# A two-layer attention encoder on one core: layer A's queries and group 0's keys transposed by VectorE in 32x32 blocks through DRAM, products with v moved between the projections

## The chip, the cores and the metric

The kernel runs on one core of a Trainium2 chip. The metric is the device time of one execution in microseconds (us), as a median of several runs. All matrix work is on TensorE (PE). VectorE (DVE), ScalarE (ACT) and GpSimd (POOL) work beside it, and SyncE (SP) issues almost all DMA transfers.

## The reference, cut to what matters

The input x has 512 tokens of 1024 features, float32. Two layers follow each other, A and then B. Each one normalises x, projects it, applies attention with 16 heads of 64, multiplies by silu of a gate, projects back and adds to x. Layer A, which the change is about, has three dilation groups with queries, keys and values of their own:

```python
proj = hn @ w_in                                     # 1024 -> 3 groups * (q, k, v) * 1024, and a gate of 1024
for g, (window, dilation) in enumerate(((128, 1), (512, 4), (2048, 16))):
    q = rms_norm(qkv[:, :, g, 0], q_gain[g])         # per head, over its 64 elements
    k = rms_norm(qkv[:, :, g, 1], k_gain[g])
    o, lse = dilated_group_attention(q, k, v, bias, dilation, reach)   # q.k/8 + bias, exp, times v
alpha = jax.nn.softmax(jnp.stack(lses), axis=0)      # groups are merged by their denominators
y = jnp.sum(alpha[..., None] * jnp.stack(outs), axis=0) * jax.nn.silu(gate)
x = x + y @ w_out
```

Layer B has one set of queries, keys and values and a two-dimensional neighbourhood; the change leaves it as it is.

## The kernel before, in words

**Numbers.** Every large product is done three times, with operands split in a high and a low part of type float32r (`mm3`, L212). Weights are streamed from DRAM in loads of up to 1024 columns (`raws`, L166, three buffers) and split on the chip: ScalarE casts the high part, VectorE or GpSimd subtracts the low part (`split`, L124, four buffers of each). One such split feeds 12 matmuls of 512 columns.

**Layer A** runs over 8 head pairs (`hc`, L1033). For each pair `main_a` (L474) gives PE, in this order: a projection "rawk" of 512 columns (keys of groups 1 and 2, values of groups 1 and 2), a projection "rawq" of 512 columns (queries of groups 0, 1, 2 and keys of group 0), then v of group 0 and the gate, 128 columns each, which come out transposed already (`project_t`). The first two projections are 96 matmuls each, the last two 24 each. The last pair has rawq ahead of rawk, and the gate of pair 6 is done in pair 7.

In "rawq" and "rawk" tokens lie on partitions: 4 blocks `i` of 128 tokens, and in each the columns. ScalarE evacuates each block with the row's scale (L428), GpSimd squares it (L268), VectorE sums (L269), and the reciprocal root is found by Newton steps, on VectorE for rawq and on GpSimd for rawk. VectorE scales each block in place (`scale`, L281); for rawq of pairs 0 to 5 that is held back in `later` until the gate has been evacuated (L459).

Scores need queries and keys with the head's elements on partitions. `transpose4` (L295) has PE transpose four 128x128 blocks into a PSUM bank. `k_a` (L486) does it twice a pair for the keys of groups 1 and 2. `q_a` (L497) does it four times, for q0, k0, q1 and q2: q0 and k0 are copied and split in high and low parts by ScalarE and VectorE, q1 and q2 are copied by VectorE (L514).

`attn_a` (L656) then forms the scores of a pair in two halves (`scores(u)`), with softmax on VectorE and ScalarE. For all pairs but the last, the softmax weights are transposed off PE already: VectorE transposes them in blocks of 32x32 into the buffer `tr` (L636), four DMAs write that to DRAM and four read it back in another order into `pt` (`turner`, L625). The products with v of a pair (`weigh`, L736) are held in `pending` and done during the next pair, after its first half of scores.

**The order of the work.** PE's order is the program's own. `main` gives the projections, and after each few matmuls `run` (L798) lets `side` emit a piece of attention when it is due: a `yield "wait", key, n` makes the next piece due n ns after the time stamped for that key, counted on a clock of PE's work (`clock`, L198). `later_on` (L226) emits DMAs after a delay on the same clock. A scheduler orders the other engines' instructions, save those that are pinned to the program's order (`keep_in_program_order`). SP's DMAs, weight loads among them, go out one after the other, and one that waits holds up those behind it.

Of the kernel before, what the change touches and what calls it, by code (L numbers as in the profile page):

```python
# [13 lines left out]
F32 = mybir.dt.float32  # L14
F32R = mybir.dt.float32r
I32 = mybir.dt.int32
AF = mybir.ActivationFunctionType
# [25 lines left out]
def tile_hybrid_encoder(  # L43
# [231 lines left out]
    def head_norm(raw, ss, ns, held):  # L275


        rs = wk.tile([P, 32], F32, tag="rs", name="rs")
        rsqrt(nc.vector if ns == 8 else nc.gpsimd, rs[:, : 4 * ns], ss[:, : 4 * ns], 4 * ns, 1.0 / DH)

        def scale():  # L281
            for i in range(4):
                v = raw[:, i, : ns * 64].rearrange("p (a b) -> p a b", b=64)
                m = nc.vector.tensor_mul(
                    v, v, rs[:, i * ns : (i + 1) * ns].unsqueeze(2).to_broadcast([P, ns, 64])
                )
# [16 lines left out]
    def to_tjr(t):  # L303
        return t.rearrange("p (j t r) -> p t j r", t=4, j=4)
# [103 lines left out]
    pq = wk.tile([P, 4096], F32, tag="pt", name="pt", bufs=1)  # L408
    rk = wk.tile([P, 4608], F32, tag="rawk", name="rawk", bufs=1)

    def project_qk(n, ns, key, hc, guard, first=False, **kw):

        box = []

        def evac(i, acc):
            if not box:
                q = key == "rawq"
                if q:
                    box.append(wk.tile([P, 4, n], F32, tag="rawq", name=key, bufs=1))
                else:  # L420
                    o = 4 * n * (hc % (2 if n == 512 else 3))
# [3 lines left out]
            if first:  # L425
                nc.scalar.copy(raw[:, i, :], acc[:, :n])
                return
            nc.scalar.activation(raw[:, i, :], acc[:, :n], AF.Copy, scale=rs_n[:, i : i + 1])  # L428
            squares(raw, ss, i, ns)

        tile_of = lambda hn: lambda k, i: hn[:, k, P * i : P * (i + 1)]
        yield from project(tile_of(hn_h), tile_of(hn_l), n, evac, guard, **kw)
        raw, ss = box
        if first:
            st["first"] = raw, ss
            return
        normed(raw, ss, ns, key, hc)

    def normed(raw, ss, ns, key, hc):
        head_norm(raw, ss, ns, key == "raw" or (key == "rawq" and hc < NHC - 2))  # L440
        st[key, hc] = raw
        stamp[key, hc] = clock[0]

    def first_out():

        raw, ss = st.pop("first")
        for i in range(4):
            nc.scalar.activation(raw[:, i, :], raw[:, i, :], AF.Copy, scale=rs_n[:, i : i + 1])
            squares(raw, ss, i, 4)
        normed(raw, ss, 4, "rawk", 0)  # L450

    def gate_a(hc):
        acc = []
        yield from project_t(acc)
        yield "ya", hc - 2, "y"
        gt = wk.tile([P, S], F32, tag="gt", name="gt", bufs=3)
        eg = wk.tile([P, S], F32, tag="eg", name="eg")
        tc.keep_in_program_order(nc.vector.tensor_mul(tjr(gt), to_tjr(acc[0]), tjr(rs_half)))
        while later:  # L459
            later.pop()()  # L460
        nc.scalar.activation(eg, gt, AF.Tanh)
        gated(hc, gt, eg)

# [20 lines left out]
            yield from gate_a(hc)  # L484

    def k_a(hc):  # L486
        yield "wait", ("rawk", hc), 12500 if hc == 0 else 16000 if hc < NHC - 1 else 10000
        k12 = wk.tile([P, 2, 512], F32, tag="k12", name="k12", bufs=1)
        raw = st.pop(("rawk", hc))
        for g in range(2):  # L490
            tp = transpose4(raw, g * P)
            nc.vector.tensor_scalar(k12[:, g, :], tp, gk[:, g + 1 : g + 2], None, op0=ALU.mult)
            yield
        st["k12", hc] = k12, raw
        stamp["k12", hc] = 0

    def q_a(hc):  # L497
        yield "wait", ("rawq", hc), 15000 if hc < NHC - 2 else 13000
        raw = st.pop(("rawq", hc))
        q0h = wk.tile([P, 512], F32R, tag="q0h", name="q0h", bufs=1)  # L500
        q0l = wk.tile([P, 512], F32R, tag="q0l", name="q0l", bufs=1)
        q12 = wk.tile([P, 2, 512], F32, tag="q12", name="q12", bufs=1)
        k0h = wk.tile([P, EXT], F32R, tag="k0h", name="k0h", bufs=1)
        k0l = wk.tile([P, EXT], F32R, tag="k0l", name="k0l", bufs=1)
        tp = transpose4(raw, 0)
        nc.scalar.copy(tjr(q0h), to_tjr(tp))
        nc.vector.tensor_sub(tjr(q0l), to_tjr(tp), tjr(q0h.bitcast(F32)))
        yield
        tp = transpose4(raw, 3 * P)
        put_k([(trj(k0h[:, 64:EXT]), trj(k0l[:, 64:EXT]), to_trj(tp))], 0)  # L510
        yield
        for g in range(2):
            tp = transpose4(raw, (g + 1) * P)
            nc.vector.tensor_copy(tjr(q12[:, g, :]), to_tjr(tp))  # L514
            yield
        st["q", hc] = q0h, q0l, q12, k0h, k0l
        stamp["q", hc] = 0

    def v_a(hc):

# [135 lines left out]
    def attn_a(hc):  # L656
# [72 lines left out]
        def turn_p(hd, t, pr):  # L729
# [3 lines left out]
            dst = sb(pts[0], at(t, 0, hd, 0), [[32, 4], [512, 4], [1, 32]])  # L733
            nc.vector.tensor_copy(dst, tp.rearrange("p (i a r) -> p i a r", i=4, a=4))

        def weigh():  # L736
            assert not any(t.left for t in turners)
            o = bank("o")
            mms = []
            for g in range(2):  # L740
                for j in range(4):
                    c = 256 + P * g
# [302 lines left out]
    def side():  # L1045
# [20 lines left out]
        for hc in range(NHC):  # L1066
            if hc < NHC - 1:
                yield from k_a(hc)
                yield from chain(q_a(hc), v_a(hc))
                yield from attn_a(hc)  # L1070
                if hc == 2:
                    bias_rows()
            else:
                gap[0] = cycle((500, 500, 700))
                yield from chain(q_a(hc), k_a(hc), attn_a(hc))
        yield from residual(xg)
        stamp["ya", KT - 1, "y"] = 0
        yield "wait", ("x", KT - 1), 800
# [105 lines left out]
```

## Time and profile before

| what | value |
|---|---|
| median of 3 runs | 861.84 us (861.52 to 864.07) |
| the profiled execution | 863.44 us, span 861.7 us |
| mean granted TensorE clock | 0.999 |
| instructions | 15492, on PE 5643 matmuls |
| layer A's share, about 0 to 530 us | one pair takes 66.0 us (200 to 266, 266 to 332) |

The profile's times are in us from the start of the span. In a group's row stand the line, engine, operation, what is written and read, shape and count, then busy time, the mean ns of one and the idle time before it. In a row of the timeline stand the start, the length, the instruction and, in brackets, how long the engine was idle before it and what ended that. In a row of the waits stand who waited for whom, the total, the number of times and the longest.

### The profile page before, as it was taken

To read this page: it belongs to the slowest core of one execution; us is meant where nothing else is said; L and a number is where in the kernel's file an instruction comes from. 1 tells how busy PE (TensorE), PEld (TensorE's weight loads), DVE (VectorE), ACT (ScalarE), POOL (GpSimd) and SP (SyncE) were. 2 spreads that over 40 slices of the span, in tenths; PEclk is the share of its full clock that TensorE was granted. 3 is DMA by queue.
4 is the path that set the end of the run, shared out by engine and by line. 5 is a ranking of instruction groups with operands and counts; after the bars stand their busy time and mean duration, and the time that the engine had idled before them with its cause. 6 is when DMAs were issued, how large, how long until landed. Compare 5 with 4: busy or idle time off the path is not lost.

```text
span 861.7 us, 15492 instructions
## 1 busy us (share of the span) xinstructions
PE 854.2 (99%) x5643; PEld 712.2 (83%) x5643; DVE 513.3 (60%) x1323; ACT 423.1 (49%) x880; POOL 296.2 (34%) x493
## 2 busy tenths in 40 slices
PE   8999999999999999999999999999999999999998
PEld 6788888788788788788788788789988899889786
DVE  6445666566476566566466775538466656766642
ACT  7432653553553553553552564435466645665541
POOL 2351441441541432442342432112444335542411
PEclk9999999999999999999999999999999999999999
DMA  7343565564465464465465274265235664656223
GB/s 247 110 131 108 150 170 157 159 178 137 138 202 156 125 200 130 133 192 148 129 171 175 84 229 105 65 197 179 95 113 149 180 168 145 167 160 174 99 96 124
DMA packets 59707, 128.64 MB, mean 149 GB/s; under 512 B 6384, under 2 KB 23728, under 8 KB 59632
## 3 DMA queue, kind: packets, MB, share of 16 engines
q1 hardware_dynamic: 59344, 127.66, 49.3%
q8 instruction: 44, 0.72, 0.4%
q14 instruction: 31, 0.25, 0.1%
q10 hardware_dynamic: 288, 0.01, 0.0%
HBM read 102.82 MB, written 24.83 MB: 148 GB/s over the span
## 4 chain that ended last, share of the span: by engine, by line
PE 97%; ACT 1%; DVE 1%; DMA 1%; issue 0%; ACTq 0%; DVEq 0%
PE acc L206 82%; PE log L206 5%; PE o L206 5%; PE tp L210 4%; DMA hg<-in_head_gain 1%; ACT p L976 1%; DVE hn_l L368 0%; ACT p L564 0%; ACT rawk L428 0%; ACT wh L127 0%; PE pa L206 0%; PE pl L206 0%; PE pk L206 0%; DVE wl L131 0%; DVE pt L889 0%
## 5 line engine op out<-in xcount | busy, mean ns | idle before, releaser
L127 ACT CAST wh<-wraw 128x512 fp32r<-128x512 f32 (+1 forms) x276 | 161.6, 587 | 298.1 <-PE acc L206 247.4
L206 PE MATMUL acc<-wh,hn_h 128*128 128x512 f32 (+1 forms) x768 | 296.5, 386 | 0.8 <-ACT wh L127 0.7
L206 PE MATMUL acc<-wh,hn_l 128*128 128x512 f32 (+1 forms) x768 | 286.6, 373 | 0.0
L206 PE MATMUL acc<-wl,hn_h 128*128 128x512 f32 (+1 forms) x768 | 286.1, 373 | 0.4 <-DVE wl L131 0.4
L131 POOL TENSOR_TENSOR wl<-wraw,wh 128x512 fp32r<-128x512 f32 (+1 forms) x110 | 137.7, 1252 | 392.9 <-ACT wh L127 342.2
L131 DVE TENSOR_TENSOR wl<-wraw,wh 128x512 fp32r<-128x512 f32 (+1 forms) x166 | 113.2, 682 | 141.5 <-ACT wh L127 137.0
L206 PEld LDWEIGHTS acc<-wh,hn_h 128*128 128x128 f32 x768 | 144.6, 188 | 27.4 <-issue 5.5
L206 PEld LDWEIGHTS acc<-wh,hn_l 128*128 128x128 f32 x768 | 144.6, 188 | 21.1
L206 PEld LDWEIGHTS acc<-wl,hn_h 128*128 128x128 f32 x768 | 144.9, 189 | 19.0 <-DVE wl L131 0.9
L206 PE MATMUL acc<-hn_h,wh 128*128 128x512 f32 x192 | 76.9, 400 | 0.2
L206 PE MATMUL acc<-hn_h,wl 128*128 128x512 f32 x192 | 74.9, 390 | 0.0
L206 PE MATMUL acc<-hn_l,wh 128*128 128x512 f32 x192 | 74.8, 390 | 0.0
L725 ACT ACTIVATE p<-p,mn 128x512 f32<-128x512 f32 (+1 forms) x64 | 44.8, 700 | 53.9 <-DVE mn L714 53.9
L564 ACT ACTIVATE p<-p,mn 128x512 f32<-128x512 f32 (+3 forms) x128 | 69.1, 586 | 0.0
L269 DVE TENSOR_REDUCE ss<-sq 128x4 f32<-128x256 f32 (+1 forms) x96 | 48.4, 504 | 27.3 <-POOL sq L268 26.8
L636 DVE STREAM_TRANSPOSE tr<-p 128x512 f32<-128x512 f32 (+1 forms) x80 | 54.1, 688 | 12.1 <-ACT p L564 10.0
L268 POOL TENSOR_TENSOR sq<-rawk 128x256 f32<-128x256 f32 x64 | 40.5, 640 | 40.5 <-ACT rawk L428 33.5
L206 PE MATMUL acc<-y_h,wh 128*128 128x512 f32 x128 | 52.2, 408 | 0.0
L206 PE MATMUL acc<-y_h,wl 128*128 128x512 f32 x128 | 50.0, 390 | 0.0
L206 PE MATMUL acc<-y_l,wh 128*128 128x512 f32 x128 | 50.0, 390 | 0.0
L206 PEld LDWEIGHTS acc<-hn_h,wh 128*128 128x128 f32 x192 | 36.1, 188 | 9.8 <-ACT rawk L428 2.1
L206 PEld LDWEIGHTS acc<-hn_h,wl 128*128 128x128 f32 x192 | 36.0, 188 | 7.7
(131 smaller groups left out, 1077.8 us busy)
## 6 DMA issues: line engine op xcount, KB each, us to landing
wraw<-in_w SPq DMA_DIRECT2D x95, 512.0 KB
wraw<-in_w SPq DMA_DIRECT2D x38, 384.0 KB
td<-tr SPq DMA_DIRECT2D x56, 256.0 KB
pt<-td SPq DMA_DIRECT2D x56, 256.0 KB
td<-tr SPq DMA_DIRECT2D x24, 224.0 KB
pt<-td SPq DMA_DIRECT2D x24, 224.0 KB
e<-l_d SPq DMA_DIRECT2D x32, 112.0 KB
e<-l_d SPq DMA_DIRECT2D x16, 128.0 KB
```

What stands on the lines that cost most here:

```text
L127: nc.scalar.copy(h, raw)
L131: eng.tensor_sub(l, raw, h.bitcast(F32))
L206: nc.tensor.matmul(o, l, r, **kw)
L210: nc.tensor.transpose(o, i, ident)
L268: nc.gpsimd.tensor_mul(sq, raw[:, i, : ns * 64], raw[:, i, : ns * 64])
L269: nc.vector.tensor_reduce(ss[:, i * ns : (i + 1) * ns], sq.rearrange("p (a b) -> p a b", b=64), axis=AX.X, op=ALU.add)
L564: nc.scalar.activation(pr, pr, AF.Copy, scale=mn[:, 3:4])
L636: nc.vector.transpose(dst, src[:, :n].rearrange("p (i b k) -> p i b k", b=4, k=32))
L725: nc.scalar.activation(row, row, AF.Exp, bias=mn[:, 1:2], scale=-1.0, accum_out=mn[:, 2:3])
L976: nc.scalar.activation(pr[:, o : o + n], pr[:, o : o + n], AF.Exp, bias=mn[:, 0:1], scale=-1.0, accum_out=mn[:, 2:3])
```

## The change

Layer A's rawq is no longer transposed by PE. It is evacuated into a tile of another layout (16 blocks of 32 columns, then 4 blocks of tokens, then 32), scaled at once, and VectorE transposes its 32x32 blocks in place, one instruction for each block of tokens. Four DMAs write the tile to DRAM in pieces of 512 bytes, one for each 32 partitions, and four read back k0, q0, q1 and q2 with the head's elements on partitions. `split_q` then makes the high and low parts of q0 and k0; q1 and q2 are read straight into their place. Group 0's key gain and the factor for q0 change sides: q0 is now scaled by `gk`, k0 is copied. rawk is evacuated in two pieces, keys into a single buffer and values of groups 1 and 2 into one of three. The gate is copied out of PSUM by ScalarE and scaled by VectorE from the copy. The times at which pieces are due are set anew: a pair's first scores stand later (27 us and two steps after its rawq, on the clock), and the products with v of the pair before stand between the next rawk and rawq projections.

```diff
-    def squares(raw, ss, i, ns):
+    def squares(v, ss, i, ns):
         sq = wk.tile([P, 512], F32, tag="sq", name="sq")[:, : ns * 64]
-        nc.gpsimd.tensor_mul(sq, raw[:, i, : ns * 64], raw[:, i, : ns * 64])
+        nc.gpsimd.tensor_mul(sq.rearrange("p (c r) -> p c r", r=32) if ns == 8 else sq, v, v)
...
+                if ns == 8:
+                    v = raw[:, :, i, :].rearrange("p (a b) r -> p a b r", b=2)
+                    by = by.unsqueeze(3).to_broadcast([P, ns, 2, 32])
...
+                if key == "rawq":
+                    box.append(wk.tile([P, 16, 4, 32], F32, tag="rawq", name=key, bufs=1))
+                elif key == "rawk":
+                    box.append(part(0))
+                    st["v12", hc] = part(1 + hc % 3)
...
+            if key == "rawq":
+                pieces = [(raw[:, :, i, :], acc.rearrange("p (c r) -> p c r", r=32))]
+            elif key == "rawk":
+                pieces = [(raw[:, i, :], acc[:, :256]), (st["v12", hc][:, i, :], acc[:, 256:])]
...
     def normed(raw, ss, ns, key, hc):
-        head_norm(raw, ss, ns, key == "raw" or (key == "rawq" and hc < NHC - 2))
+        head_norm(raw, ss, ns, key == "raw")
+        if key == "rawq":
+            turn_q(raw)
...
-        tc.keep_in_program_order(nc.vector.tensor_mul(tjr(gt), to_tjr(acc[0]), tjr(rs_half)))
-        while later:
-            later.pop()()
+        nc.scalar.copy(tjr(gt), to_tjr(acc[0]))
+        nc.vector.tensor_mul(gt, gt, rs_half)
...
-        yield "wait", ("rawk", hc), 12500 if hc == 0 else 16000 if hc < NHC - 1 else 10000
+        yield "wait", ("rawk", hc), 12500 if hc == 0 else 25500 if hc == 1 else 18500 if hc < NHC - 1 else 10000
...
+    def turn_q(raw):
+        for i in range(4):
+            nc.vector.transpose(raw[:, :, i, :], raw[:, :, i, :])
...
     def q_a(hc):
-        yield "wait", ("rawq", hc), 15000 if hc < NHC - 2 else 13000
+        yield "wait", ("rawq", hc), 15000 if hc != 1 else 18000
         raw = st.pop(("rawq", hc))
+        d = dr.tile([16, 32, 4, P], F32, name="qd", tag="qd", bufs=2)
+        q12 = wk.tile([P, 2, 512], F32, tag="q12", name="q12", bufs=1)
+        k0, q0 = (wk.tile([P, 512], F32, tag="eg", name="q0") for _ in range(2))
+        lands, left = ((3, k0), (0, q0), (1, q12[:, 0, :]), (2, q12[:, 1, :])), [4]
+
+        def write(t):
+            src = raw[32 * t : 32 * t + 32].rearrange("k c i r -> k c (i r)")
+            tc.keep_in_program_order(nc.sync.dma_start(d[:, :, t, :].rearrange("c k x -> k c x"), src))
+            if t == 3:
+                stamp["q", hc] = 0
+
+        def read(f, dst):
+            src = d[4 * f : 4 * f + 4].rearrange("a k t x -> (a k) (t x)")
+            tc.keep_in_program_order(nc.sync.dma_start(dst, src))
+            left[0] -= 1
+
+        for n in range(4):
+            later_on(700 * n, partial(write, n))
+            later_on(6800 + 700 * n, partial(read, *lands[n]))
+        def land():
+            yield "wait", ("rawq", hc), 27000 if hc != 1 else 30000
+            assert not left[0]
+            st["q", hc] = split_q(q0, k0, q12)
+            yield
...
+    def split_q(q0, k0, q12):
...
-        tp = transpose4(raw, 0)
-        nc.scalar.copy(tjr(q0h), to_tjr(tp))
-        nc.vector.tensor_sub(tjr(q0l), to_tjr(tp), tjr(q0h.bitcast(F32)))
-        yield
-        tp = transpose4(raw, 3 * P)
-        put_k([(trj(k0h[:, 64:EXT]), trj(k0l[:, 64:EXT]), to_trj(tp))], 0)
-        yield
-        for g in range(2):
-            tp = transpose4(raw, (g + 1) * P)
-            nc.vector.tensor_copy(tjr(q12[:, g, :]), to_tjr(tp))
-            yield
+        nc.scalar.copy(trj4(k0h), src)
+        put_k([(q0h, q0l, q0)], 0)
+        nc.vector.tensor_sub(trj4(k0l), src, trj4(k0h.bitcast(F32)))
...
+        def weighed():
+            yield "wait", ("rawk", hc + 1), 0
+            pending.pop(0)()
+            yield
...
-                if u == 0:
-                    yield 1200
+                if u == 0 and hc:
+                    yield 600
+                elif hc == 0:
+                    yield "wait", ("rawk" if u == 0 else "rawq", 1), 0
                 elif hc < NHC - 2:
-                    yield "wait", ("rawk", hc + 1), 6500
+                    yield "wait", ("rawk", hc + 1), 10000
...
-                later_on(9000, partial(turned.send, pq[:, 2048 * u : 2048 * u + 2048], 11000, 1500))
-                if pending and u == 0:
-                    yield 2500
-                    pending.pop(0)()
+                later_on(7500, partial(turned.send, pq[:, 2048 * u : 2048 * u + 2048], 11000, 1500))
+                if 0 < hc < NHC - 2 and u == 0:
+                    yield from weighed()
```

More of the change, by code (lines that the diff above doesn't have):

```diff
@@ L282, in scale @@
             for i in range(4):
[L283 to L286, printed above, removed]
+                by = rs[:, i * ns : (i + 1) * ns].unsqueeze(2)
+                if ns == 8:
+                    v = raw[:, :, i, :].rearrange("p (a b) r -> p a b r", b=2)
+                    by = by.unsqueeze(3).to_broadcast([P, ns, 2, 32])
+                else:
+                    v = raw[:, i, : ns * 64].rearrange("p (a b) -> p a b", b=64)
+                    by = by.to_broadcast([P, ns, 64])
+                m = nc.vector.tensor_mul(v, v, by)
                 if held:
@@ L409, in tile_hybrid_encoder, with part @@
     rk = wk.tile([P, 4608], F32, tag="rawk", name="rawk", bufs=1)
+    def part(n):
+        return rk[:, 1024 * n : 1024 * n + 1024].rearrange("p (i c) -> p i c", i=4)
     def project_qk(n, ns, key, hc, guard, first=False, **kw):
@@ L416, in evac @@
             if not box:
-                q = key == "rawq"
-                if q:
-                    box.append(wk.tile([P, 4, n], F32, tag="rawq", name=key, bufs=1))
+                if key == "rawq":
[3 more added lines that the diff above has]
+                    st["v12", hc] = part(1 + hc % 3)
                 else:
-                    o = 4 * n * (hc % (2 if n == 512 else 3))
+                    o = 4 * n * (hc % 3)
                     box.append(rk[:, o : o + 4 * n].rearrange("p (i c) -> p i c", i=4))
@@ L424, in evac @@
             raw, ss = box
[L425 to L429, printed above, removed]
+            if key == "rawq":
+                pieces = [(raw[:, :, i, :], acc.rearrange("p (c r) -> p c r", r=32))]
+            elif key == "rawk":
+                pieces = [(raw[:, i, :], acc[:, :256]), (st["v12", hc][:, i, :], acc[:, 256:])]
+            else:
+                pieces = [(raw[:, i, :], acc[:, :n])]
+            for dst, src in pieces:
+                if first:
+                    nc.scalar.copy(dst, src)
+                else:
+                    nc.scalar.activation(dst, src, AF.Copy, scale=rs_n[:, i : i + 1])
+            if not first:
+                squares(raw[:, :, i, :] if ns == 8 else raw[:, i, : ns * 64], ss, i, ns)
         tile_of = lambda hn: lambda k, i: hn[:, k, P * i : P * (i + 1)]
@@ L447, in first_out @@
         for i in range(4):
-            nc.scalar.activation(raw[:, i, :], raw[:, i, :], AF.Copy, scale=rs_n[:, i : i + 1])
-            squares(raw, ss, i, 4)
+            for t in (raw, st["v12", 0]):
+                nc.scalar.activation(t[:, i, :], t[:, i, :], AF.Copy, scale=rs_n[:, i : i + 1])
+            squares(raw[:, i, :], ss, i, 4)
         normed(raw, ss, 4, "rawk", 0)
@@ L493, in k_a @@
             yield
-        st["k12", hc] = k12, raw
+        st["k12", hc] = k12, st.pop(("v12", hc))
         stamp["k12", hc] = 0
+    def turn_q(raw):
+        for i in range(4):
+            nc.vector.transpose(raw[:, :, i, :], raw[:, :, i, :])
     def q_a(hc):
-        yield "wait", ("rawq", hc), 15000 if hc < NHC - 2 else 13000
+        yield "wait", ("rawq", hc), 15000 if hc != 1 else 18000
         raw = st.pop(("rawq", hc))
+        d = dr.tile([16, 32, 4, P], F32, name="qd", tag="qd", bufs=2)
[19 more added lines that the diff above has]
+            yield
+        st["land", hc] = land()
@@ L500, in q_a @@
+    def split_q(q0, k0, q12):
         q0h = wk.tile([P, 512], F32R, tag="q0h", name="q0h", bufs=1)
         q0l = wk.tile([P, 512], F32R, tag="q0l", name="q0l", bufs=1)
-        q12 = wk.tile([P, 2, 512], F32, tag="q12", name="q12", bufs=1)
         k0h = wk.tile([P, EXT], F32R, tag="k0h", name="k0h", bufs=1)
         k0l = wk.tile([P, EXT], F32R, tag="k0l", name="k0l", bufs=1)
-        tp = transpose4(raw, 0)
-        nc.scalar.copy(tjr(q0h), to_tjr(tp))
-        nc.vector.tensor_sub(tjr(q0l), to_tjr(tp), tjr(q0h.bitcast(F32)))
@@ L508, in q_a @@
-        yield
-        tp = transpose4(raw, 3 * P)
-        put_k([(trj(k0h[:, 64:EXT]), trj(k0l[:, 64:EXT]), to_trj(tp))], 0)
-        yield
-        for g in range(2):
-            tp = transpose4(raw, (g + 1) * P)
-            nc.vector.tensor_copy(tjr(q12[:, g, :]), to_tjr(tp))
-            yield
-        st["q", hc] = q0h, q0l, q12, k0h, k0l
-        stamp["q", hc] = 0
+        src = k0.rearrange("p (t j r) -> p t r j", t=4, j=4)
+        trj4 = lambda t: t[:, 64:EXT].rearrange("p (t r j) -> p t r j", t=4, j=4)
@@ L519, in v_a @@
+        nc.scalar.copy(trj4(k0h), src)
+        put_k([(q0h, q0l, q0)], 0)
+        nc.vector.tensor_sub(trj4(k0l), src, trj4(k0h.bitcast(F32)))
+        return q0h, q0l, q12, k0h, k0l
     def v_a(hc):
@@ L741, in weigh @@
                 for j in range(4):
-                    c = 256 + P * g
+                    c = P * g
                     mms.append((
@@ L1069, in side @@
                 yield from chain(q_a(hc), v_a(hc))
-                yield from attn_a(hc)
+                if hc == NHC - 2:
+                    yield "wait", ("rawq", hc + 1), 0
+                    pending.pop(0)()
+                yield from chain(st.pop(("land", hc)), attn_a(hc))
                 if hc == 2:
@@ L1074, in side @@
                 gap[0] = cycle((500, 500, 700))
-                yield from chain(q_a(hc), k_a(hc), attn_a(hc))
+                yield from chain(q_a(hc), k_a(hc))
+                yield from chain(st.pop(("land", hc)), attn_a(hc))
         yield from residual(xg)
```

## The prediction

> **What bounds the kernel now.** I read the page first: engine shares and the chain that ended last.
>
> ```profile
> span 861.7 us, 15492 instructions
> PE 854.2 (99%) x5643; PEld 712.2 (83%) x5643; DVE 513.3 (60%) x1323; ACT 423.1 (49%) x880; POOL 296.2 (34%) x493
> PEclk9999999999999999999999999999999999999999
> PE 97%; ACT 1%; DVE 1%; DMA 1%; issue 0%; ACTq 0%; DVEq 0%
> ```
>
> TensorE is the chain, at full clock. A busy PE proves little by itself, as ends of matmuls are modelled, so next come its waits. This is the whole list:
>
> ```profile
> PE busy L346 <- DVE warm L335: 1.5, 1, 1.5
> PE acc L206 <- ACT wh L127: 0.7, 1, 0.7
> PE acc L206 <- DVE wl L131: 0.4, 1, 0.4
> PE tp L210 <- ACT p L564: 0.4, 1, 0.4
> PE o L206 <- issue: 0.3, 1, 0.3
> ```
>
> That is 3.3 us in 861.7: no other engine holds PE up anywhere, so PE work taken out shortens the run unless a new wait appears. The waits of the other engines show how far weights run ahead:
>
> ```profile
> ACT wh L127 <- PE acc L206: 247.4, 159, 4.4
> ACT wh L127 <- DMA wraw<-in_w: 6.1, 3, 3.2
> ```
>
> ScalarE's weight casts nearly always wait for PE to free a buffer (four of them, 12 matmuls each), seldom for a load. The weight stream can be late by microseconds before PE feels it.
>
> **What a removed transpose is worth.** In the group view:
>
> ```profile
> L210 PE MATMUL tp<-ident,rawq 128*128 128x128 f32 x128 | 19.2, 272 | 0.0
> ```
>
> These 128 (16 in each of 8 head pairs) disappear. Their 272 ns is a latency, overlapped with neighbours; PE's timeline gives the price, first without transposes, then around them:
>
> ```profile
> 29.98 0.39 PE L206 MATMUL acc<-wh,hn_h 128*128 128x512 f32 x1
> ...
> 33.38 0.39 PE L206 MATMUL acc<-wh,hn_h 128*128 128x512 f32 x1
> ```
> ```profile
> 72.74 0.60 PE L210 MATMUL tp<-ident,rawq 128*128 128x128 f32 x4
> ...
> 74.56 0.60 PE L210 MATMUL tp<-ident,rawq 128*128 128x128 f32 x4
> ...
> 80.06 0.60 PE L210 MATMUL tp<-ident,vt 128*128 128x128 f32 x4
> ```
>
> From 29.98 to 33.38 are 15 matmuls: 0.2267 us each. From 72.74 to 80.06 are four groups of four transposes and 24 matmuls: 7.32 - 24 x 0.2267 = 1.88 us, or 0.47 a group. Eight head pairs x 1.88 = **15.0 us** removed. The other PE work (keys' transposes, scores, products with v) keeps its counts in the built order and only changes place.
>
> [...]
>
> **What is added, and its cover.** VectorE loses two copies and gains four transposes a pair; the gate's product stays, and its PSUM copy goes to ScalarE.
>
> ```profile
> L636 DVE STREAM_TRANSPOSE tr<-p 128x512 f32<-128x512 f32 (+1 forms) x80 | 54.1, 688 | 12.1 <-ACT p L564 10.0 <-DMA pt<-td 1.4 <-POOL p L700 0.4
> L514 DVE COPY q<-tp 128x512 f32<-128x512 f32 x16 | 11.0, 687 | 5.9 <-PE tp L210 5.9
> ```
> ```profile
> 200.00:266.00 66.00, 66.00 (x469) 53.70 (x468) 39.74 (x100) 31.20 (x57) 23.93 (x40) 1.00 0.54 160
> ```
>
> That is 4 x 0.69 - 2 x 0.69 = +1.4 us on VectorE's 39.7 of a pair's 66.0 us (columns: PE, PEld, DVE, ACT, POOL), about +1 on ScalarE's 31.2. Neither becomes the bound; cost 0. Each pair also moves 1 MB out and 1 MB back on a queue at a share of 0.54.
>
> What can cost is the **round trip**. I follow pair 3 from the end of its query projection, t = 0 at 251.5 us (the last of four evacuations starts there).
>
> ```profile
> 249.44 2.73 ACT L428 ACTIVATE rawq<-acc,rs_n 128x512 f32<-128x512 f32 x4
> 261.49 0.19 DVE L116 SCALAR_TENSOR_TENSOR rs<-na,rs 128x32 f32<-128x32 f32 x1
> 262.97 2.49 DVE L284 TENSOR_TENSOR rawq<-rawq,rs 128x512 f32<-128x512 f32 x4
> ```
>
> The norm is ready at 261.7. In the built order VectorE now does four scalings (2.5), four transposes (4 x 0.65 back to back), one weight split and the gate's product (0.65 each): done at 268.1, t = 16.7. The first DRAM write stands on SP behind a weight load whose buffer frees when PE has done v's and the gate's projections (48 x 0.2267 = 10.9) and the next cast and split (1.5): t = 12.4. So SP waits some 4 us for the last transpose. Behind the write stands the next weight load, and its buffer frees 24 matmuls later, t = 17.8: nothing is lost. The writes issue until t = 18.4. How long they take is not in the trace (pieces of 512 B). Nearest is a load with three 256 KB writes in pieces of 2 KB:
>
> ```profile
> 220.80 0.33 SPq L175 DMA_DIRECT2D wraw<-in_w  x1
> 221.42 1.32 SPq L645 DMA_DIRECT2D td<-tr  x3
> ```
> ```profile
> DMA  0000000789896979999999962000000000000399
> ```
> ```profile
> q1 hardware_dynamic: 59344, 127.66, 49.3%
> ```
> ```profile
> q1 hardware_dynamic: 341, 0.33, 27.3%
> ```
>
> The digits (220 to 230 us, 0.25 us each) show data from 221.75 to 226.5: 1 us after the first issue, 3.8 us after the last, at 1.31 MB / 4.75 us. By bytes our four writes land at t = 22.2. Dearer bounds go by packets, 128 on each of 16 engines: the bias loads between 306 and 310 us (0.97 KB each) give 0.273 x 16 x 4 us / 341 = 51 ns, so 6.5 us and t = 24.2; the whole run's mean (2.15 KB) 0.493 x 16 x 861.7 us / 59344 = 115 ns, so 14.7 us and t = 32.4. The cheapest bound, below by-bytes, gains nothing, since the scores come no earlier. From 2.15 to 0.97 KB the cost falls with size, so I take by-bytes.
>
> The reads of k0 and q0 issue at 22.3 to 23.1 and, with a weight load ahead, land 3.8 us later, t = 26.9. ScalarE splits (0.58 + 0.69), VectorE follows (0.68 + 0.75): t = 29.6. Groups 1 and 2 are read behind the next weight load and land by t = 29. The scores that need all this come, in the built order, after 48 + 24 + 63 = 135 matmuls and v's transposes: 135 x 0.2267 + 0.47 = **t = 31.1**. Margin: 1.5 us. Pairs 2 to 5 have this margin; 0, 1 and 6 have the scores 3 us later (pair 1's VectorE is busier, which takes it back); pair 7 has far more. ScalarE stands still for k0 from t = 22.4 to about 27; weight casts behind it start 2 to 3 us late, covered by their lead.
>
> **The moved work.** The first half's scores now stand nine matmuls before the end of the next key projection, so exponentials and the keys' evacuation (eight halves instead of four) meet on ScalarE.
>
> ```profile
> 280.97 0.67 ACT L725 ACTIVATE p<-p,mn 128x448 f32<-128x448 f32 x1 [1.96 <-DVE mn L714]
> ```
> ```profile
> 283.19 1.97 PE L206 MATMUL o<-pt,rawk 128*64 128x128 f32 x32
> 284.99 1.90 PE L206 MATMUL o<-pt,v 128*64 128x256 f32 x16
> 286.81 0.50 PE L206 MATMUL acc<-wh,hn_h 128*128 128x512 f32 x1
> ```
>
> The first exponential starts 2.7 us after the scores (278.24, row below). With 0.67 for an exponential of 448 columns (0.71 for 512, an estimate), 0.6 for a normalisation and 0.39 for a half evacuation (an estimate from 0.69 for a whole), the order "two halves, two exponentials, two halves, ..." frees the last accumulator 9.0 us after the scores start. PE wants it at 10.0: 2.2 scores, 2.0 nine matmuls, 0.7 three more, 3.6 for the products with v (283.19 to 286.81), 1.5 for six. The products are the cover; without them PE would stand 2.6 us a pair. Cost 0, margin 1 us.
>
> The two score blocks of a pair also move together: 42 matmuls and the products between them, where 69 were, 6.1 us less. Both turn their weights in the one buffer `tr`, which the first block's four DRAM writes must have left.
>
> ```profile
> 278.24 0.36 PE L206 MATMUL log<-k0h,q0h 64*128 64x192 f32 x2
> ...
> 299.95 0.39 PE L206 MATMUL log<-k0h,q0h 64*128 64x256 f32 x2
> ```
> ```profile
> 306.68 0.71 DVE L636 STREAM_TRANSPOSE tr<-p 128x512 f32<-128x512 f32 x1 [0.45 <-DMA pt<-td]
> ```
>
> Now the second block's scores start at 299.95, 21.7 us after the first's; its first transpose came 6.7 later and waited 0.45 for a landing already. With the writes' delay cut by 1.5 us (9000 to 7500 ns), some 4.6 of the 6.1 us may come back as a wait on VectorE. Queued behind it are weight splits of steps that PE reaches 5 us later and more: cost 0, and were that lead gone, up to 5 us a pair. The keys' projection buffer is single now; its last reader, the keys' transposes, stands a whole pair ahead of the next write: 0.
>
> **The sum.** The profiled execution took 863.4 us for its 861.7 of span, 1.6 over the median of the three runs (861.84). 863.4 - 15.0 = 848.4; from the median 846.8. For margins this thin I add an estimate of 0.7, a tenth of a microsecond in each of seven pairs: **847.5 us**.
>
> **Rivals.**
> - Partly late: packets cost about the 51 ns bound, or a load ahead holds reads up, and scores stand 1 to 2 us in pairs 1 to 5. Five x 1.5 = 7.5: 854.3. For it: margins of 1 to 1.5 us. Against: by-bytes leaves room.
> - Slower: the 512-byte writes are paid by the packet. At 115 ns they land at t = 32.4, 10.2 later than taken; less 1.5 of margin, PE stands 8.7 us at the scores of pairs 2 to 5 and some 5.7 in 0, 1 and 6: 52 us, 846.8 + 52 = 899. It decides from a lateness L with 4L + 3(L - 3) = 17.6, so L = 3.8: writes of 9.1 us, 71 ns a packet. Against: the bias loads' 51 ns.
> - No gain: transposes were filling time that PE would idle in anyway: 861.8. Against: the five waits above.
> - Whole price: each transpose holds PE for its whole 272 ns, with drains that neighbours do not hide: 128 x 0.272 = 34.8 us go, 827.0. Against: the start-to-start times. [...]
>
> [...]
>
> **How the numbers follow.** Forecast (845 to 851) 0.62; partly late (851 to 861) 0.17; slower 0.14; no gain 0.05; whole price 0.02. A measurement of this kernel tells about 0.3% from no change, 859.3 to 864.4. Faster: 0.62 + 0.02 + most of partly late (0.15) = 0.79; within: 0.05 + 0.02 = 0.07; slower 0.14. The range takes in forecast and partly late with a microsecond for PE's pace: 844 to 861, leaving out 0.2.
>
> **What would show it.** Right: 128 transposes gone, matmuls at 0.227 us where they stood, PE's list of waits still under 6 us. Round trip: waits of "log" for q0h, k0l, q0l or a read of q1, q2. Evacuation: waits of "acc" for ScalarE's rawk just after the products with v. Wrong would be idle PE time of more than 2 us a pair in either place, or a write that lasts far over 1 us on its own.

## The result, and the profile after

| | before | after |
|---|---|---|
| median of 19 runs each | 862.36 us (861.43 to 865.85) | 868.32 us (863.21 to 872.74) |
| profiled execution, span | 863.44, 861.7 us | 867.95, 866.1 us |
| mean granted clock in it | 0.999 | 0.992 |

The ratio is 1.0072 (95% interval 1.0055 to 1.0089): after is 0.7% slower, where 847.5 us were forecast. Its span is 19.4 us over the 846.7 that before's span less 15.0 asks for. Line numbers from here on are those of the changed kernel. The page of after, its lines on span, engines, clock and chain:

```profile
span 866.1 us, 15411 instructions
PE 845.2 (98%) x5515; PEld 702.3 (81%) x5515; DVE 520.8 (60%) x1339; ACT 433.1 (50%) x924; POOL 304.9 (35%) x493
PEclk9999999899999999999999999999999999999999
PE 76%; DMA 9%; DVE 5%; ACT 4%; POOL 3%; issue 1%; SPq 1%; ACTq 0%; DVEq 0%; POOLq 0%
```

The 128 transposes are gone (5643 matmuls before, 5515 now), but TensorE's share of the chain fell from 97% to 76%, and one digit of the clock is an 8. One stretch of each kernel shows a pair that goes as forecast, by windows from the first scores of one pair to those of the next (us, then busy time of PE, PEld, DVE, ACT, POOL, then granted clock, DMA share, GB/s). Before, from pair 3's scores to pair 4's, and after, from pair 4's to pair 5's:

```profile
278.24:344.25 66.01, 66.01 (x469) 53.70 (x468) 39.90 (x98) 31.20 (x57) 23.04 (x36) 1.00 0.51 155
```
```profile
347.82:411.94 64.12, 64.12 (x453) 52.14 (x452) 41.74 (x100) 31.71 (x63) 23.13 (x36) 1.00 0.69 192
```

That is 1.89 us less for one pair; the forecast's price was 1.88. It is after's best pair: from pair 3's scores to pair 4's it took 64.60, with 0.2 of waits in it. What was lost stands in five places. Four of them are in TensorE's timeline in after, the instructions ahead of which it stood (in brackets how long, and what ended it):

```profile
151.48 0.53 PE L206 MATMUL log<-k0h,q0h 64*128 64x192 f32 x2 [4.22 <-ACT q0h L578]
...
475.45 0.50 PE L206 MATMUL acc<-wh,hn_h 128*128 128x512 f32 x1 [2.40 <-ACT rawq L444]
...
508.11 0.80 PE L206 MATMUL acc<-hn_h,wh 128*128 128x512 f32 x1 [2.33 <-ACT rawk L444]
...
523.83 0.33 PE L210 MATMUL tp<-ident,rawk 128*128 128x128 f32 x1 [3.09 <-DVE rawk L290]
```
```profile
PE acc L206 <- ACT gt L478: 1.8, 2, 1.6
```

The last line, of after's waits (total, times, longest), is the fifth: 1.6 us in pair 3 at 263, with 0.2 more in pair 4. The first is pair 1, the others are pairs 6 and 7. Together 13.8 us. After three of them the granted clock was halved (windows of after, from where PE went on):

```profile
151.48:156.20 4.72, 4.67 (x78) 3.73 (x79) 3.76 (x13) 2.42 (x6) 1.47 (x2) 0.50 0.36 116
...
508.10:511.20 3.10, 3.10 (x7) 2.51 (x8) 2.43 (x6) 2.65 (x7) 2.85 (x5) 0.50 0.61 170
524.90:528.30 3.40, 3.40 (x11) 2.81 (x12) 2.52 (x4) 0.00 (x0) 0.24 (x1) 0.50 0.78 229
```

If half the clock is half the pace, half of these 11.2 us, 5.6, is lost as well (an estimate: for the first piece it gives 2.4, and the experiment on the clock below measured 2.0). 13.8 + 5.6 = 19.4, the whole of it; that it agrees to the tenth is luck.

The waits of ScalarE name a common source (who, for whom: total, times, longest):

```profile
ACT k0h L559 <- DMA q<-qd: 36.1, 8, 6.9
ACT wh L127 <- DMA wraw<-in_w: 33.6, 10, 6.9
```

In every pair ScalarE stands 4.5 us on average before k0's cast, until its read has landed; before there was no such wait, and 6.1 us for weight loads instead of 33.6. What that does is seen in pair 1, first in SP's timeline, then ScalarE's:

```profile
133.31 3.27 SPq L532 DMA_DIRECT2D qd<-rawq  x4
136.69 1.11 SPq L175 DMA_DIRECT2D wraw<-in_w  x1
137.84 1.94 SPq L694 DMA_DIRECT2D pt<-td  x3
139.99 0.34 SPq L538 DMA_DIRECT2D q<-qd  x1
140.38 0.56 SPq L694 DMA_DIRECT2D pt<-td  x1
141.03 0.46 SPq L175 DMA_DIRECT2D wraw<-in_w  x1
141.53 3.15 SPq L538 DMA_DIRECT2D q<-qd  x3
```
```profile
148.06 1.06 ACT L559 CAST k0h<-q 128x512 fp32r<-128x512 f32 x1 [6.88 <-DMA q<-qd]
149.03 0.62 ACT L127 CAST wh<-wraw 128x512 fp32r<-128x512 f32 x1
150.71 0.72 ACT L578 ACTIVATE q0h<-q,gk 128x512 fp32r<-128x512 f32 x1 [1.07 <-DMA q<-qd]
```

Four reads of pair 0's softmax weights (`pt<-td`) and two weight loads share SP and the queue with the four reads of pair 1's queries. k0 was issued at 139.99 and its cast began at 148.06; the scores wanted all at 147.1.

At the end of pair 6 the scores are not late at all. There the cast that stands holds up something else:

```profile
472.60 1.08 ACT L559 CAST k0h<-q 128x512 fp32r<-128x512 f32 x1 [4.32 <-DMA q<-qd]
473.59 0.72 ACT L578 ACTIVATE q0h<-q,gk 128x512 fp32r<-128x512 f32 x1
474.22 0.60 ACT L127 CAST wh<-wraw 128x512 fp32r<-128x512 f32 x1
474.73 1.82 ACT L444 ACTIVATE rawq<-acc,rs_n 128x512 f32<-128x512 f32 x3
```

The evacuation of pair 7's queries is behind it in ScalarE's order, and TensorE waits for that accumulator. At 520 us the way is longer. ScalarE's timeline, GpSimd's, then VectorE's:

```profile
516.07 1.14 ACT L559 CAST k0h<-q 128x512 fp32r<-128x512 f32 x1 [5.32 <-DMA q<-qd]
...
518.27 0.61 ACT L127 CAST wh<-wraw 128x512 fp32r<-128x512 f32 x1
```
```profile
518.96 1.83 POOL L131 TENSOR_TENSOR wl<-wraw,wh 128x512 fp32r<-128x512 f32 x1 [4.47 <-ACT wh L127]
520.76 0.64 POOL L119 TENSOR_SCALAR na<-na 128x16 f32<-128x16 f32 x1
```
```profile
523.34 1.43 DVE L290 TENSOR_TENSOR rawk<-rawk,rs 128x256 f32<-128x256 f32 x4
```

k0's cast holds up a weight cast (the two rows of ScalarE), this GpSimd's split of the same weights, the split the Newton steps of pair 7's keys behind it, these VectorE's scaling and that the keys' transposes.

### The profile page after: what moved, and what is told of

It reads as the page before. It is cut to its first block, busy times and chain, and to the rows that moved or that the text cites. A ratio compares the mean times of both kernels' runs of the same rounds, so it can differ in the third digit from the quotient of the medians.

```text
span 866.1 us, 15411 instructions
## 1 busy us (share of the span) xinstructions
PE 845.2 (98%) x5515; PEld 702.3 (81%) x5515; DVE 520.8 (60%) x1339; ACT 433.1 (50%) x924; POOL 304.9 (35%) x493
## 4 chain that ended last, share of the span: by engine, by line
PE 76%; DMA 9%; DVE 5%; ACT 4%; POOL 3%; issue 1%; SPq 1%; ACTq 0%; DVEq 0%; POOLq 0%
PE acc L206 64%; PE log L206 4%; PE o L206 4%; DMA wraw<-in_w 3%; DMA q<-qd 3%; PE tp L210 3%; DMA qd<-rawq 1%; DMA e<-l_d 1%; POOL wl L131 1%; POOL sq L268 1%; DVE rawq L519 1%; DVE rawq L290 1%; DMA pt<-td 1%; ACT wh L127 1%; ACT rawq L444 1%
## 5 line engine op out<-in xcount | busy, mean ns | idle before, releaser
L206 PE MATMUL acc<-wh,hn_h 128*128 128x512 f32 (+1 forms) x768 | 293.3, 382 | 4.4 <-ACT rawq L444 2.4
L131 POOL TENSOR_TENSOR wl<-wraw,wh 128x512 fp32r<-128x512 f32 (+1 forms) x110 | 141.1, 1283 | 389.5 <-ACT wh L127 367.2
L131 DVE TENSOR_TENSOR wl<-wraw,wh 128x512 fp32r<-128x512 f32 (+1 forms) x166 | 116.8, 704 | 116.2 <-ACT wh L127 111.9
L268 POOL TENSOR_TENSOR sq<-rawk 128x256 f32<-128x256 f32 x64 | 42.7, 675 | 64.9 <-ACT rawk L444 51.9
```

Of the source, the lines that this page charges most:

```text
L131: eng.tensor_sub(l, raw, h.bitcast(F32))
L206: nc.tensor.matmul(o, l, r, **kw)
L268: nc.gpsimd.tensor_mul(sq.rearrange("p (c r) -> p c r", r=32) if ns == 8 else sq, v, v)
```

## The experiments

**Theory 1**: the sum is right, and the loss is the late round trip, passed on by engines that stand in order, with the clock on top. **Theory 2**: the added traffic itself starves the weight loads. **Theory 3**: the moved work costs. The kernel before was run beside each experiment, and ratios are to those runs.

### The round trip without its wait, and without its traffic

```diff
-            st["q", hc] = split_q(q0, k0, q12)
+            f = raw.rearrange("p c i r -> p (c i r)")
+            st["q", hc] = split_q(f[:, 0:512], f[:, 512:1024], hn_h[:, 2:4, :].bitcast(F32))
```

> After as it is, with all eight DMAs of the round trip of every pair, but what they bring is not used: the parts of q0 and k0 are made from the tile as it stands after VectorE's transposes, and q1 and q2 come from the normalised x. So nothing waits for the reads (the output is not the reference's). Theory 1 (the round trip lands late; ScalarE, in order, stands before k0's cast and holds up evacuations and weight casts, and PE's stalls also halve its clock for a while): the stalls of after at 147 us (4.6), 472 (2.8) and 520 (3.5) go, with them half of some 10 us at half clock; 852 us, between 849 and 855. Theory 2 (the added traffic fills the DMA queue and starves the weight loads): the traffic is the same, so 865 to 868. Theory 3 (the moved products, the evacuation in halves and the gate's copy cost): also 865 to 868.

Measured: 853.7 us, ratio 0.9887 (0.9871 to 0.9904). The stalls of pair 1, at 472 and at 520 are gone. The one of 505 is left, and a new one has come at 525, for reads of softmax weights (mean clock 0.995; 0.997 in the next kernel, which has no such stall):

```profile
PE o L206 <- DMA pt<-td: 2.1, 1, 2.1
```

ScalarE's weight casts still waited 27.4 us for loads in this run (33.6 in after), and PE's only wait for weights was 0.6 us. For the rest, the second kernel takes the eight DMAs of a pair out too:

```diff
-            tc.keep_in_program_order(nc.sync.dma_start(d[:, :, t, :].rearrange("c k x -> k c x"), src))
...
-            tc.keep_in_program_order(nc.sync.dma_start(dst, src))
```

> The first experiment (nothing waits for the round trip, the output is not the reference's) with the eight DMAs of every pair taken out as well. If the 7 us that it kept over the 847 of the sum are the added traffic (late weight loads and late writes of the softmax weights): 846 to 849. If they are the moved work: 852 to 855 as with the traffic.

Measured: 852.33 us, 0.9883 (0.9868 to 0.9898), so the traffic costs at most some 2 us when nothing waits for it (the stall at 525 is gone here); theory 2 falls as the main cause. One wait over 0.5 us is left once PE has started, in this kernel's waits:

```profile
PE acc L206 <- ACT rawk L444: 3.0, 1, 3.0
```

It is the stall of 505. With it goes 1.6 of clock (an estimate: half of the 3.10 us that after ran at 0.50 there; the mean clock here is 0.997). It stays without any round trip, so no read causes it: pair 6's second half of scores, 11 us after the first, puts its exponentials ahead of the evacuation of pair 7's keys. Without the transposes PE also comes to the end of the keys sooner, 30 matmuls after those scores; the kernel of the next experiment has 36 and four groups of transposes there, and doesn't wait. The profiled execution took 852.88; less 4.6 it is 848.3. So the sum of the prediction (847.5) was right for a kernel in which nothing waits.

### The moved work alone

All eight pairs by PE (`q_pe` is `q_a` of before), nothing through DRAM, everything else as in after:

```diff
-        if key == "rawq":
+        if key == "rawq" and not (hc >= 0):
             turn_q(raw)
...
+        if hc >= 0:
+            yield from q_pe(hc)
+            return
```

> After with everything that it moves (products with v between the projections, evacuation of the keys in halves, the gate's copy, the due times), but PE transposes q0, k0, q1 and q2 in all eight pairs as before, and nothing goes through DRAM for them. Theory 1: no late round trip and no gain, so about before, 861 to 865. Theory 2: the same, 861 to 865. Theory 3: the loss of 20 us without the gain of 15, so 875 to 883.

Measured: 868.44 us, 1.0067 (1.0052 to 1.0082): 3 us over what theories 1 and 2 expected, far under theory 3. The waits of this kernel:

```profile
PE acc L206 <- ACT rawk L448: 4.3, 5, 0.9
```

In five pairs the queries' projection waits for the keys' evacuation. Here the scores stand 27 matmuls ahead of the keys' end in pairs 2 to 5, in after 12, and ScalarE's order has exponentials ahead of the evacuation. The next kernel only shifts them (`27000` to `29600`, pair 1 `30000` to `32600`):

> The moved work alone (all pairs by PE, no round trip) with the scores of pairs 1 to 5 2.7 us later, which puts them 12 to 15 matmuls ahead of the end of the next keys as in after. If the 5 us came from exponentials ahead of the keys' evacuation on ScalarE: 861 to 864. If the moved work costs whatever its place: 867 to 869.

Measured: 863.69 us, 1.0020 (1.0010 to 1.0029), and those five waits are gone. So the moved work is nearly free in pairs 1 to 5, as forecast, but only with ScalarE's order just so, as after has it there.

### The reads ahead in the queue

```diff
-later_on(7500, partial(turned.send, pq[...], 11000, 1500))
+later_on(7500, partial(turned.send, pq[...], 11000 if u == 0 or hc > 4 else 28000 if hc else 18500, 1500))
```

> After with one edit: the four reads of the softmax weights of a pair's second half are issued behind the reads of the next pair's queries instead of ahead of them (pair 0 by 7.5 us later, pairs 1 to 4 by 17). Theory 1a (in pair 1 the reads of k0 and q0 stand on SP and in the DMA queue behind those reads, and at 250 to 262 us the same reads make a weight load late): the stall of pair 1 falls from 4.6 us to under 1.5 with its 1.7 of clock, and the 2.0 of pair 3 goes: 860 to 863 against 868.3. Theory 1b (pair 1 is late because VectorE ends its transposes at 20.9 us after the projection instead of 16.7, whatever stands in the queue): pair 1's stall stays above 3 us, and 866 to 868 comes out.

Measured: 888.47 us, 1.0303 (1.0268 to 1.0338). The delay was right for pair 0 and wrong for pairs 1 to 4, whose reads landed among the next pair's query reads instead of behind them. So the run tests both directions. Pair 1, where they went behind, then pair 2, where they went between; SP's timeline for pair 2 first:

```profile
205.12 1.33 SPq L175 DMA_DIRECT2D wraw<-in_w  x1
206.49 1.03 SPq L694 DMA_DIRECT2D pt<-td  x1
208.51 0.81 SPq L538 DMA_DIRECT2D q<-qd  x2
209.37 0.43 SPq L694 DMA_DIRECT2D pt<-td  x1
209.91 0.39 SPq L175 DMA_DIRECT2D wraw<-in_w  x1
210.34 0.91 SPq L538 DMA_DIRECT2D q<-qd  x2
```
```profile
147.77 0.36 PE L206 MATMUL log<-k0h,q0h 64*128 64x192 f32 x2 [0.39 <-ACT q0h L578]
...
216.63 0.35 PE L206 MATMUL log<-k0h,q0h 64*128 64x192 f32 x2 [1.11 <-ACT q0h L578]
...
219.73 0.68 PE L206 MATMUL log<-k,q 64*32 64x128 f32 x16 [1.22 <-DMA q<-qd]
```

Pair 1's first scores came at 147.77 instead of 151.48 (the scores of pair 0 within 0.2 us in both runs). But PE then stood before pair 0's products with v, which need the delayed reads:

```profile
156.26 0.98 PE L206 MATMUL o<-pt,rawk 128*64 128x128 f32 x14 [2.71 <-DVE ss L269]
```

The row names VectorE's sum, which ended just then; the packets of the delayed reads ran until 155.6. Which of the two it was is not shown. Pairs 2 to 5, whose scores had no wait in after, stood some 3 us each at the scores, by the waits for the scores (13.7 us in the run, 1.4 of them in pair 1): 69.6 us from pair 3's scores to pair 4's, at a mean clock of 0.98, where after had 64.6; over the run the clock is 0.986, 0.992 in after. Theory 1a holds: which reads go first decides whether the scores wait. In pair 1 much of the gain went into the wait before the products.

The same for pair 1 by an earlier second half of pair 0 (`"wait", ("rawk", 1), 15000 * u`):

> After with one edit: pair 0's second half of scores 8 us earlier, so that its reads lie ahead of pair 1's query writes. Theory 1a: pair 1's stall (4.6 and 1.7 of clock) falls to under 1.5; all else stays: 861 to 863. Theory 1b (VectorE's late transposes): the stall stays above 3: 867 or so.

Measured: 865.49 us, 1.0034 (1.0015 to 1.0054). Pair 1's wait for q0h fell to 0.3 us or less, but two new ones came (0.9 for the queries' evacuation at 115, 2.0 before the products with v at 155; mean clock 0.994), so it gained about half of what was expected.

### Who stands

```diff
-        nc.scalar.copy(trj4(k0h), src)
-        put_k([(q0h, q0l, q0)], 0)
+        nc.vector.tensor_copy(trj4(k0h), src)
+        nc.vector.tensor_scalar(q0h, q0, gk[:, 0:1], None, op0=ALU.mult)
+        nc.vector.scalar_tensor_tensor(q0l, q0, gk[:, 0:1], q0h.bitcast(F32), op0=ALU.mult, op1=ALU.subtract)
```

> After with one edit: the high parts of k0 and q0 are made by VectorE instead of ScalarE (about 1.3 us a pair more on VectorE), so ScalarE no longer stands before a read of the round trip. Theory 1 (ScalarE's standing in order passes the lateness on): the stall at 472 (2.8, an evacuation behind k0's cast) and that at 520 (3.5 and 1.7 of clock, a weight cast behind it) go, that of pair 1 stays since its scores need the data themselves: 860 to 862. Theory 2 (loads starved by traffic): no change, 867 to 869. If VectorE, which stands before the same reads, is as harmful a place: 868 or more.

Measured: 870.93 us, 1.0114 (1.0088 to 1.0140). The stall at 472 is gone, as expected; that of 520 grew to 6.2 us and pair 1's to 5.6. My expectation for 520 missed: here VectorE was no better a place to stand than ScalarE.

The gate's product on VectorE again, as before:

> After with one part undone: the gate leaves PSUM by VectorE's product as before, not by ScalarE's copy. Theory 1: the 2.0 us at 263 (gate's accumulator waits for ScalarE, which stands before a late weight load) go, nothing else: 866 to 867. Theory 3 (the gate's copy is one of the moved works that cost): the same or 1 us more in other pairs. If the copy is not what holds that accumulator: 868.

Measured: 867.32 us, 1.0073 (1.0046 to 1.0100). The 1.6 us at 263 went, but three waits for VectorE's gate (3.0) came; the copy on ScalarE is not what costs.

### The clock

```diff
+            if hc == 1 and u == 0:
+                for n_ in range(18):
+                    nc.tensor.matmul(tiles[0][1][0], ones[:, :P], ones, start=True, stop=True)
```

> After with 18 matmuls of 512 columns more (4.1 us of work whose result is overwritten) on PE just ahead of pair 1's first scores, where PE stood 4.6 us. Theory 1 on the clock (an idle PE is what halves it): PE doesn't stand, the 6.8 us at half clock after it go, and the run gets 3 us shorter although work was added, about 865 against 868. If the clock does not hang on the stall: same as after or longer by what exceeds the wait, 868 to 869.

Measured: 868.02 us, 1.0049 (1.0029 to 1.0069), not to be told from after by the total; the 3 us less that were expected did not come. In the stretch itself it shows. From pair 1's first scores to its second, after took 17.18 us; the filled kernel's window:

```profile
153.99:169.49 15.50, 15.18 (x165) 11.72 (x165) 11.50 (x34) 11.31 (x25) 8.96 (x22) 1.00 0.36 128
```

With PE kept busy the clock stayed at 1.00, and the same work took 1.7 us less, with 0.3 us of waits still in it: 2.0 us for half the clock. Elsewhere in that run pair 3's stall was 2.0 us (1.6 in after), and the mean clock rose only from 0.992 to 0.994, where pair 1's 6.83 us at half clock are worth 0.004: other pieces at half clock came instead.

### Mends

```diff
-            yield "wait", ("rawq", hc), 27000 if hc != 1 else 30000
+            yield "wait", ("rawq", hc), {1: 30000, 6: 31000, 7: 36000}.get(hc, 27000)
...
-                    yield 11000
+                    yield 17000
...
-        nc.scalar.copy(trj4(k0h), src)
+        keep(nc.scalar.copy(trj4(k0h), src))
```

`keep` pins the casts of k0 and q0 to the program's order in pair 6. A fourth edit (`16800` to `22000`) makes pair 6's products with v due 5.2 us later. The first version also has the reads of the softmax weights moved as in the experiment on the queue.

> After with the mends that theory 1 asks for: the reads of the softmax weights later as in the run before last; pair 6's scores 4 us later and k0's cast of that pair behind the evacuation of pair 7's queries; its second half of scores behind the end of pair 7's keys (17 us after the first instead of 11); pair 7's parts of q0 and k0 9 us later. Theory 1: the stalls of pair 1, of 472, 505 and 520 shrink to 2 us together and the clock stays full: 849 to 854. Theory 2: the traffic is the same, 862 or more.

Measured: 883.12 us, 1.0261 (1.0235 to 1.0288), since it held the misplaced reads of pairs 1 to 4. Without them, and with pair 0's second half earlier as above:

> After with these mends, and the reads of the softmax weights of pairs 1 to 5 left where after has them: pair 0's second half of scores 8 us earlier (15 us after pair 1's keys instead of at the end of its queries), so that its four reads lie ahead of pair 1's query writes; pair 6's scores 4 us later, with k0's cast of that pair behind the evacuation of pair 7's queries; pair 6's second half 17 us after its first; pair 7's parts of q0 and k0 9 us later. Theory 1: of after's 20 us, pair 1 (4.6 and 1.7), 472 (2.8), 505 (2.7 and 1.7) and 520 (3.5 and 1.7) go to within 3 us; pair 3's 2.0 stays: 848 to 853. Theory 2 (traffic): 860 or more.

Measured: 861.93 us, 0.9989 (0.9977 to 1.0001). The stalls of 472, 505 and 520 are gone and pair 1's is small, yet eight round trips give no more than before, far from the 848 to 853 expected. In its best execution, the profiled one (858.09 us, span 856.3), PE's waits after its start come to 9.7 us (1.8 in before), none over 1.7: for reads, for the gate's copy and before products above all. They make up most of what lies over 846.7. Of its twelve executions only one more was as fast (858.45); why the others took 859.7 to 864.1, at clocks of 0.994 to 0.998, no trace here shows. Giving the tightest pairs back to PE (`hc in (1, 6, 7)` in place of `hc >= 0` in the edit of the moved work alone):

> After, but in pairs 1, 6 and 7 PE transposes as before; pairs 0 and 2 to 5 go through DRAM. Theory 1: five of eight parts of 15.0, 9.4 us, are gained; the stalls at 147, 472 and 520 go; the 2.0 at 263 stays, and perhaps the 2.7 at 505: 853 to 858. Theory 2: pairs 2 to 5 starve as in after, 858 to 863. Theory 3: 866 to 872.

Measured: 858.49 us, 0.9950 (0.9935 to 0.9965), half a microsecond over what theory 1 expected and within what theory 2 did, so this run alone does not decide between them. With `hc > 5` and pair 0's second half earlier:

> After with pair 0's second half 8 us earlier, and pairs 6 and 7 transposed by PE; pairs 0 to 5 through DRAM. Theory 1: 3.8 us of the 15.0 are given back, and the stalls of pair 1, 472, 505 and 520 are gone but for 1 to 2 us: 852 to 857.

Measured: 859.49 us, 0.9969 (0.9953 to 0.9985): worse than expected, as pair 0's earlier half brought the two waits told above. The last takes the kernel with pairs 1, 6 and 7 by PE and shifts pair 1's scores (`30000` to `32600`):

> The version with pairs 1, 6 and 7 by PE (858.5), with one mend: pair 1's scores 2.7 us later, so that ScalarE evacuates keys between its exponentials as in pairs 2 to 5. Theory 1: the 1.1 us at 153 go; the two waits for the gate's copy (2.2) and 1.5 for reads stay: 857, between 855.5 and 858.5; faster than both kernels.

Measured: 856.37 us, 0.9927 (0.9913 to 0.9940), **faster than both kernels**, by 0.7% against before and with the clock at full. The page's clock and its whole list of waits from 0.5 us on:

```profile
PEclk9999999999999999999999999999999999999999
```
```profile
PE busy L350 <- DVE warm L339: 1.4, 1, 1.4
PE acc L206 <- ACT gt L482: 1.1, 2, 0.9
PE tp L210 <- DVE mn L799: 0.9, 1, 0.9
```

## Why the prediction was wrong

- **The price of the transposes** was right: 1.89 us a pair against 1.88 where nothing waits, and 848.3 against 847.5 with the round trip and one stall left out. "Whole price" and "no gain" fall.
- **The writes of 512 bytes** were little trouble. In the packet records of after, one took 33 ns on average (the dearer bounds were 51 and 115), and a 256 KB write landed 3.7 us after its issue (median of 32). From the first issue to the last landing a pair's four took 6.0 to 7.3 us, where the sum had 5.5: SP needed 3.1 to 4.7 us to issue them, and the sum had 1.7. The slower rival had the right sign by the wrong mechanism. In the median a packet of 512 B took 27 ns, 19 bytes per ns on one engine, and one of 2 KB 84 ns, 24 bytes per ns.
- **The step that failed and cost most** is "ScalarE stands still for k0 from t = 22.4 to about 27; weight casts behind it start 2 to 3 us late, covered by their lead". The standing was right (4.5 us a pair), and weight casts mostly were covered; but in pair 6 an evacuation stands behind it, and in pair 7 a chain over GpSimd and VectorE. I had followed pair 3 and not asked what else is behind the cast where the last pair's order differs. By the prices above that is 2.4 us at 472 and 3.1 with 1.7 of clock at 520, 7.2 of the 19.4.
- **The margins** failed with it: "0, 1 and 6 have the scores 3 us later (pair 1's VectorE is busier, which takes it back); pair 7 has far more". In pair 1 the transposes did end late (20.9 us after the projection instead of 16.7, by the timeline), but the reads of pair 0's softmax weights in the same queue were not in the sum, and the reads that were to "land 3.8 us later" took 8.1 us for k0 (139.99 to 148.06). Moving those of the softmax weights alone took the scores' stall away, though 2.7 us before the products came instead. With its clock this stall is 6.6 of the 19.4. "A load ahead holds reads up" stood in the rival "partly late", which put it in pairs 1 to 5 at 1 to 2 us. In after it was pair 1 alone, with 4.2.
- **The moved work**, "Cost 0, margin 1 us", held in pairs 1 to 5 (with twelve matmuls behind the scores in pairs 2 to 5, where the sum had nine) but was never worked out for pairs 6 and 7, where the same meeting of exponentials and evacuation, at pair 6's second half, costs 2.3 us in after and 3.0 without the round trip, with 1.6 of clock by the estimate above.
- **No term for the clock.** A stall was priced at its length. Here 13.8 us of stalls brought some 5 to 5.6 more.
- Pair 3's 1.6 us was not forecast: ScalarE stood 6.9 us before a weight cast, until the load had landed at 263.1, with the gate's copy behind it, in a stretch with bias loads and both halves' traffic. No run of its own takes it apart, so its cause stays open.

## What to carry to other kernels

Before work is taken off a saturated engine, list every place where an engine will stand for the new transfer (here ScalarE, 4.5 us a pair before k0's cast), and what is queued behind each of them, in the first and last rounds of the loop above all, where the order differs. Price a transfer with what is ahead of it in the same queue: k0's read of 256 KB took 8.1 us in pair 1, and its lateness went when other reads were moved. Where those go counts as much: among the next queries' reads they cost some 3 us a pair, and more by the clock (0.986 against 0.992). A mixed version that keeps the old way where there is no slack can beat both, as here.

## What the runs showed of the hardware

In after three pieces of the run were granted half the clock (0.50): 6.83 us from 149.42, 3.41 us from 507.82 and 3.41 us from 524.89. Each lies at a stall of TensorE: the first sets in 2.06 us before the end of that of 4.22 us in pair 1, the second 0.29 before the end of that of 2.33 at 505, the third 1.06 after that of 3.09 at 520. In the kernel with pairs 6 and 7 by PE one of 2.02 us has half the clock behind it, shown here with the window that follows:

```profile
156.89 0.55 PE L206 MATMUL o<-pt,rawk 128*64 128x128 f32 x6 [2.02 <-issue]
```
```profile
157.90:161.10 3.20, 3.20 (x26) 2.78 (x24) 2.96 (x11) 2.86 (x8) 1.35 (x7) 0.50 0.20 76
```

The 2.40 us at 473 in after have none: the clock is 1.00 from 156.25 to 507.82. So the length of these stalls alone does not say which of them cost more than their length, and what else does is left open. After's times spread wider too: 863.2 us at a mean clock of 0.996 and 872.7 at 0.988, against 861.4 to 865.9 for before.
